# Experts: the activation issued behind the down projection's weights, and its 1 + tanh added on ScalarE

## The chip, the cores and the metric

The kernel runs on one core of a Trainium2 chip. The metric is the device time of one execution in microseconds (us). Five engines work side by side, each through its own row of instructions: TensorE (PE, matmuls; PEld are its weight loads), VectorE (DVE), ScalarE (ACT), GpSimd (POOL) and SyncE (SP, whose queue issues most transfers). An instruction waits by semaphores for what it needs, and whatever stands behind it on its engine waits with it.

## What is computed

The reference is two transformer blocks on 512 tokens of width 1024. The first has a layer of 32 experts, of which each token goes to 4; the change lies there. Cut to that:

```python
def expert_block(args):
    xblk, e = args
    gu = xblk @ w_gate_up[e] + b_gate_up[e]                 # [slots, 2048]
    gate = jnp.minimum(gu[:, :D_FF], SWIGLU_LIMIT)          # limit 7
    up = jnp.clip(gu[:, D_FF:], -SWIGLU_LIMIT, SWIGLU_LIMIT)
    act = (up + 1.0) * (gate * jax.nn.sigmoid(SWIGLU_ALPHA * gate))   # alpha 1.702
    return act @ w_down[e] + b_down[e]
...
out = jnp.zeros((t, d)).at[tbuf].add(ybuf * wbuf[:, None])
```

All of it is in float32, D_FF is 1024.

## The kernel before

**Products.** A float32 product is made of three matmuls (`mm3`, L82 to L84): both factors are split into a high and a low part, and high times low, low times high and high times high are summed in one bank of PSUM. A split is two instructions (`split`, L49 and L50): ScalarE copies the source to the high part (`whi`, `exh`), VectorE subtracts it from the source (`wlo`, `exl`). `ath` and `atl` are the same for the activation (L52, L53). So each weight tile passes through ScalarE, then VectorE, then TensorE.

**An expert.** Up to 96 token slots. Its weights are 12 tiles of 128x2048 (1 MB each), fetched by the SP queue into 8 raw buffers (L106), split into 4 buffers for high and 4 for low parts; each tile is 12 matmuls of 512 columns. An expert goes in two halves of the hidden width. A half has four tiles for its gate and up banks, here called a and b (the gate bank) and c and d (the up bank), each bank begun with a bias matmul (`add_bias`, L856), and then two tiles of a down product: in the first half of expert e that of the second half of expert e - 1 (called Yp0 and Yp1 here), in the second half that of its own first half (Yq0, Yq1). The loop over e in `moe` gives this order.

**The activation**, per half, at the end of `gate_up` (`g` is the gate bank): ScalarE makes `sg` = Relu(7 - g) (L889) and the Tanh of it (L890); VectorE clamps `up` (L893) and `gm` = min(g, 7) (L894), makes (sg + 1) * gm (L895) and (up + 1) * that (L896). sigmoid is had from the Tanh, and the factor 0.5 comes in at `ath`. Four transposes (`T<-ident,up`, L899) turn the result for the down product.

**Tokens.** `place` makes a one-hot matrix for an expert (`poh`, L772), four small matmuls give its token numbers (`T<-V`, L784, `gi` L785), four give its gates (`T<-VG`, L789; L791 copies two columns, L792 adds them). GpSimd gathers the tokens (`gather`, L796), `prep` transposes and splits them (L872, L49, L50). After an expert's last down tile ScalarE scales its two banks by the gates (`y`, L918) and GpSimd adds them to the output (`X`, L1009).

**What sets the order.** The engines take their instructions in a fixed order, found when the kernel is built: a scheduler with a modelled timeline takes what is ready by then, and what was written earlier in the text has precedence. So the order of the built program may differ from that of the text.

Of the kernel before, what the change touches and what calls it, by code (L numbers as in the profile page):

```python
# [9 lines left out]
F32 = mybir.dt.float32  # L10
# [4 lines left out]
AF = mybir.ActivationFunctionType  # L15
ALU = mybir.AluOpType
AX = mybir.AxisListType
# [12 lines left out]
NS = 96  # L30
# [4 lines left out]
def f(t):  # L35
    return t.bitcast(F32)


class Kern:
# [736 lines left out]
    def slots(self, bank, oh, V, vg, gi, gate):  # L776

        nc = self.nc
        n = oh.shape[-1]
        p = bank[:n, :4]  # L780

        def find():
            for i in range(NT):
                nc.tensor.matmul(p[:, :2], lhsT=oh[:, i], rhs=V[:, i], start=i == 0, stop=i == NT - 1)  # L784
            return nc.vector.tensor_scalar(gi[:n], p[:, 0:1], BASE, self.spare[:n], op0=ALU.add, op1=ALU.min).ins  # L785

        def gates():
            for i in range(NT):
                nc.tensor.matmul(p[:, 2:], lhsT=oh[:, i], rhs=vg[:, i], start=i == 0, stop=i == NT - 1)  # L789
            g = self.small.tile([128, 2], F32, name="g2")  # L790
            nc.vector.tensor_copy(g[:n], p[:, 2:])  # L791
            nc.vector.tensor_add(gate[:n], g[:n, 0:1], g[:n, 1:2])  # L792
        return find, gates

    def gather(self, e):
        self.nc.gpsimd.indirect_dma_start(out=self.xg[e % 2], out_offset=None, in_=self.XN[:, :],  # L796
                                          in_offset=bass.IndirectOffsetOnAxis(ap=self.gi[:NS, e:e + 1], axis=0),
                                          bounds_check=S - 1, oob_is_err=False)

    def moe_setup(self):  # L800

        nc, tc, a = self.nc, self.tc, self.a
        FF = 1024
        T = dict(reuse_waits="tile")
        self.ms = ExitStack()
        mc = self.mc = self.ms.enter_context(tc.tile_pool(name="mc", bufs=1, **T))
        xg = self.xg = [mc.tile([NS, D], F32, name=f"xg{n}") for n in range(2)]
        for t in xg:
            nc.gpsimd.memset(t, 0.0)
        self.mraw = self.ms.enter_context(tc.tile_pool(name="mraw", bufs=NE, **T))  # L810

        bias = self.bias = mc.tile([128, FF], F32R, name="bias")
        bt = self.mraw.tile([128, 2048], F32, name="bt", tag="raw")[:, :FF]
        for r in (0, 32):
            nc.sync.dma_start(bt[r:r + 32], a["b_gate_up"][:, :FF])
            nc.sync.dma_start(bt[64 + r:96 + r], a["b_gate_up"][:, FF:])
        nc.scalar.activation(bias, bt, AF.Copy)
        for r in (32, 96):  # L820
            nc.vector.tensor_sub(bias[r:r + 32], bt[r:r + 32], f(bias)[r:r + 32])

        esel = self.esel = mc.tile([128, 2, 32], F32R, name="esel")
        nc.gpsimd.memset(f(esel), 0.0)
        for r in range(0, 128, 32):
            nc.vector.tensor_copy(esel[r:r + 32, r // 64], self.ident[r:r + 32, r:r + 32])
        c7 = self.c7 = mc.tile([128, 2], F32, name="c7")
        nc.vector.memset(c7[:, 0:1], 7.0)
        nc.vector.memset(c7[:, 1:2], 0.851 * 7.0)
        self.gi = mc.tile([128, 32], I32, name="gi")  # L830
        self.gate = mc.tile([128, 32], F32, name="gate")

# [7 lines left out]
    def moe(self, ctx):  # L840


        nc, tc, a, mc = self.nc, self.tc, self.a, self.mc
        esel, bias, c7, xg = self.esel, self.bias, self.c7, self.xg
        E = 32
# [3 lines left out]
        mp = P("mp", 2, **T)  # L849
        self.wp, self.wk = (self.mraw, P("mhi", 4, **T), P("mlo", 4, **T)), 4  # L850
        psG, psY, psT = P("psG", 4, space=PSUM, **T), P("psY", 2, space=PSUM, **T), P("psTm", 2, space=PSUM, **T)
        gi, gate, gather = self.gi, self.gate, self.gather
        wgu, wdn = a["w_gate_up"], a["w_down"]

        def add_bias(ps, e, c):
            nc.tensor.matmul(ps, lhsT=esel[:, c // 2, e:e + 1].to_broadcast([128, NS]),  # L856
                             rhs=bias[:, c % 2 * 512:c % 2 * 512 + 512], start=True, stop=False)

        def place(e):

            for g in self.slots(psT.tile([128, 512], F32, name="T", tag="T"), self.onehot(mp, e), self.V,
                                self.VG[:, :, e], gi[:, e:e + 1], gate[:, e:e + 1]):
                g()

        def prep(e):
            xh = mp.tile([128, KT, NS], F32R, name="exh")
            xl = mp.tile([128, KT, NS], F32R, name="exl")
            for b in range(2):
                p = psT.tile([128, 512], F32, name="T", tag="T")[:, :4 * NS].rearrange("p (k s) -> p k s", k=4)
                for k in range(4):  # L870
                    c = (4 * b + k) * 128
                    nc.tensor.transpose(p[:, k], xg[e % 2][:, c:c + 128], self.ident[:NS, :NS])  # L872
                sl = slice(4 * b, 4 * b + 4)
                self.split(xh[:, sl], xl[:, sl], p)
            self.prep_dve = self.last_dve.ins
            return xh, xl

        def gate_up(e, h, x):
            xh, xl = x
            ps = []  # L880
            for c in (h, 2 + h):
                W = self.weight(wgu[e, :, c * 512:c * 512 + 512], KT, 512)
                p = psG.tile([128, 512], F32, name="G")[:NS]
                add_bias(p, e, c)
                self.mm3(p, [((xh[:, k], xl[:, k]), W[k]) for k in range(KT)], start=False)
                ps.append(p)
            s = mp.tile([NS, 512], F32, name="sg", bufs=3)

            nc.scalar.activation(s, ps[0], AF.Relu, scale=-1.0, bias=c7[:NS, 0:1])  # L889
            nc.scalar.activation(s, s, AF.Tanh, scale=-0.851, bias=c7[:NS, 1:2])  # L890
            u = mp.tile([NS, 512], F32, name="up", bufs=3)
            g = mp.tile([NS, 512], F32, name="gm", bufs=2)
            nc.vector.tensor_scalar(u, ps[1], 7.0, -7.0, op0=ALU.min, op1=ALU.max)  # L893
            nc.vector.tensor_scalar(g, ps[0], 7.0, None, op0=ALU.min)  # L894
            nc.vector.scalar_tensor_tensor(s, s, 1.0, g, op0=ALU.add, op1=ALU.mult)  # L895
            self.act_dve = nc.vector.scalar_tensor_tensor(u, u, 1.0, s, op0=ALU.add, op1=ALU.mult).ins  # L896
            p = psT.tile([128, 512], F32, name="T", tag="T")[:, :4 * NS].rearrange("p (k s) -> p k s", k=4)
            for k in range(4):
                nc.tensor.transpose(p[:, k], u[:, k * 128:(k + 1) * 128], self.ident[:NS, :NS])  # L899
            th = mp.tile([128, 4, NS], F32R, name="ath", bufs=3)  # L900
            tl = mp.tile([128, 4, NS], F32R, name="atl", bufs=3)
            self.split(th, tl, p, 0.5)
            return th, tl
# [3 lines left out]
        def down(e, h, t):  # L907
            th, tl = t
            if h == 0:
                yp[e] = [psY.tile([128, 512], F32, name="Y")[:NS] for c in range(2)]  # L910
            for c in range(2):
                W = self.weight(wdn[e, h * 512:h * 512 + 512, c * 512:c * 512 + 512], 4, 512,
                                parts=2 if e == E - 1 else 1)
                self.mm3(yp[e][c], [((th[:, k], tl[:, k]), W[k]) for k in range(4)], start=h == 0, stop=h == 1)
            if h == 1 and e < E - 1:
                y = mp.tile([NS, D], F32, name="y", bufs=1)
                for c in range(2):
                    nc.scalar.activation(y[:, c * 512:c * 512 + 512], yp[e][c], AF.Copy, scale=gate[:NS, e:e + 1])  # L918
                self.scatter(y, gi[:NS, e:e + 1])
# [31 lines left out]
        x = {0: prep(0)}  # L951
        acts = {}
# [2 lines left out]
        gather(1)  # L955
        place(2)
        for e in range(E):
            acts[e, 0] = gate_up(e, 0, x[e])
            if e + 1 < E:
                x[e + 1] = prep(e + 1)  # L960
                if e + 2 < E:
                    gather(e + 2)
                if e + 3 < E:
                    place(e + 3)
            if e == E - 4:
                gates_T()
            if e == E - 2:
                one_hot()
            if e:
                down(e - 1, 1, acts[e - 1, 1])  # L970
            acts[e, 1] = gate_up(e, 1, x[e])
            if e < E - 1:
                down(e, 0, acts[e, 0])

        with tc.issue_after(self.act_dve):
            down(E - 1, 0, acts[E - 1, 0])
# [4 lines left out]
        g = gate[:NS, E - 1:E]  # L981
# [561 lines left out]
```

## Time and profile before

| | us |
|---|---|
| median of 3 runs | 3069.35 |
| lowest, highest | 3063.36, 3070.2 |
| the profiled execution | 3069.6 |
| its span in the trace | 3067.8 |

Busy shares of the span: TensorE 95%, VectorE 73%, ScalarE 56%, GpSimd 9%. The experts take the stretch from about 730 to 1840 us. In the rows below a start is in us from the span's start, followed by the duration; a bracket holds the engine's idle time ahead of the instruction and what ended it. Matmuls overlap: what one costs is the distance from its start to the next start, not its duration. The same holds in a small way for ScalarE and VectorE, where an instruction can start a little before the one ahead ends.

### The profile page before, as it was taken

To read this page: it belongs to the slowest core of one execution; us is meant where nothing else is said; L and a number is where in the kernel's file an instruction comes from. 1 tells how busy PE (TensorE), PEld (TensorE's weight loads), DVE (VectorE), ACT (ScalarE), POOL (GpSimd) and SP (SyncE) were. 2 spreads that over 40 slices of the span, in tenths; PEclk is the share of its full clock that TensorE was granted. 3 is DMA by queue.
4 is the path that set the end of the run, shared out by engine and by line. 5 is a ranking of instruction groups with operands and counts; after the bars stand their busy time and mean duration, and the time that the engine had idled before them with its cause. 6 is when DMAs were issued, how large, how long until landed. Compare 5 with 4: busy or idle time off the path is not lost. (4 is left out here: it accounts for less than half of the span.)

```text
span 3067.8 us, 39458 instructions
## 1 busy us (share of the span) xinstructions
PE 2920.2 (95%) x14226; PEld 2296.0 (75%) x14226; DVE 2245.2 (73%) x3799; ACT 1732.8 (56%) x2569; POOL 290.5 (9%) x302
## 2 busy tenths in 40 slices
PE   8999999979999999999999998999999989999998
PEld 6898878766776666666666666778787868888877
DVE  7765677669999999999999997654456675445664
ACT  5545545337777777777777774444454234444632
POOL 0000001000112111111111100011001000110100
PEclk9999999989999999999999999999999999999999
DMA  4222233469999999999999994433536533345363
GB/s 158 63 63 67 82 105 101 140 252 335 368 364 340 357 354 356 359 358 360 356 358 359 348 371 139 127 98 112 122 92 209 165 93 116 112 115 114 92 228 99
DMA packets 406409, 644.93 MB, mean 210 GB/s; under 512 B 23088, under 2 KB 150592, under 8 KB 406208
## 3 DMA queue, kind: packets, MB, share of 16 engines
q1 hardware_dynamic: 386384, 581.67, 56.8%
q0 software_dynamic: 19248, 58.58, 6.5%
q8 instruction: 114, 1.87, 0.3%
q10 hardware_dynamic: 576, 2.10, 0.2%
q14 instruction: 87, 0.71, 0.1%
HBM read 592.10 MB, written 54.36 MB: 211 GB/s over the span
## 5 line engine op out<-in xcount | busy, mean ns | idle before, releaser
L50 DVE TENSOR_TENSOR wlo<-raw,whi 128x2048 fp32r<-128x2048 f32 (+3 forms) x646 | 1166.9, 1818 | 242.0 <-ACT whi L49 236.9
L49 ACT ACTIVATE whi<-raw 128x2048 fp32r<-128x2048 f32 (+3 forms) x646 | 972.5, 1532 | 233.0 <-PE M L84 110.0
L82 PE MATMUL G<-wlo,exh 128*96 128x512 f32 x1024 | 410.1, 400 | 4.8 <-ACT exh L49 2.8
L83 PE MATMUL G<-whi,exl 128*96 128x512 f32 x1024 | 403.9, 395 | 1.9 <-DVE exl L50 1.9
L84 PE MATMUL G<-whi,exh 128*96 128x512 f32 x1024 | 403.8, 395 | 0.0
L82 PE MATMUL F<-xl,whi 128*128 128x512 f32 x768 | 312.8, 407 | 17.4 <-DVE fl L1233 11.7
L83 PE MATMUL F<-xh,wlo 128*128 128x512 f32 x768 | 307.1, 400 | 1.5 <-DVE la L94 1.0
L84 PE MATMUL F<-xh,whi 128*128 128x512 f32 x768 | 307.4, 400 | 0.0
L82 PE MATMUL M<-wlo,xh 128*128 128x512 f32 (+2 forms) x736 | 279.0, 381 | 11.1 <-ACT xh L49 3.0
L83 PE MATMUL M<-whi,xl 128*128 128x512 f32 (+2 forms) x736 | 277.1, 377 | 3.7 <-DVE xl L50 3.1
L84 PE MATMUL M<-whi,xh 128*128 128x512 f32 (+2 forms) x736 | 275.3, 375 | 0.0
L84 PEld LDWEIGHTS G<-whi,exh 128*96 128x96 f32 x1024 | 165.6, 162 | 71.5
L82 PEld LDWEIGHTS G<-wlo,exh 128*96 128x96 f32 x1024 | 165.8, 162 | 70.6 <-ACT exh L49 3.0
L82 PE MATMUL Y<-wlo,ath 128*96 128x512 f32 x512 | 207.3, 405 | 10.7 <-DVE wlo L50 10.1
L83 PEld LDWEIGHTS G<-whi,exl 128*96 128x96 f32 x1024 | 165.7, 162 | 67.3 <-DVE exl L50 2.4
L83 PE MATMUL Y<-whi,atl 128*96 128x512 f32 x512 | 202.4, 395 | 0.1
L84 PE MATMUL Y<-whi,ath 128*96 128x512 f32 x512 | 201.8, 394 | 0.0
L82 PEld LDWEIGHTS M<-wlo,xh 128*128 128x128 f32 x736 | 165.1, 224 | 32.6 <-ACT xh L49 4.9
L82 PEld LDWEIGHTS F<-xl,whi 128*128 128x128 f32 x768 | 146.8, 191 | 54.0 <-DVE fl L1233 14.9
L83 PEld LDWEIGHTS M<-whi,xl 128*128 128x128 f32 x736 | 165.9, 225 | 18.9 <-DVE xl L50 4.0
L84 PEld LDWEIGHTS M<-whi,xh 128*128 128x128 f32 x736 | 165.4, 225 | 13.7
L84 PEld LDWEIGHTS F<-xh,whi 128*128 128x128 f32 x768 | 147.0, 191 | 32.1
(474 smaller groups left out, 5047.8 us busy)
## 6 DMA issues: line engine op xcount, KB each, us to landing
raw<-in_w_gate_up SPq DMA_DIRECT2D x256, 1024.0 KB, 7.1
raw<-in_w_down SPq DMA_DIRECT2D x124, 1024.0 KB, 8.1
raw<-in_w_in SPq DMA_DIRECT2D x154, 512.0 KB, 3.9
GZ<-fl POOLq DMA_DIRECT2D x80, 256.0 KB, 2.3
raw<-in_w_out SPq DMA_DIRECT2D x24, 512.0 KB, 3.8
raw<-in_w_branch SPq DMA_DIRECT2D x24, 512.0 KB, 4.0
gt<-GZ SPq DMA_DIRECT2D x48, 256.0 KB, 3.3
raw<-in_w_in SPq DMA_DIRECT2D x32, 256.0 KB, 3.0
```

What stands on the lines that cost most here:

```text
L49: self.last_act = nc.scalar.activation(hi, src, AF.Copy)
L50: self.last_dve = (eng or nc.vector).tensor_sub(lo, src, f(hi))
L82: nc.tensor.matmul(out, lhsT=ah, rhs=bl, start=start and i == 0, stop=False)
L83: nc.tensor.matmul(out, lhsT=al, rhs=bh, start=False, stop=False)
L84: self.last_mm = nc.tensor.matmul(out, lhsT=ah, rhs=bh, start=False, stop=stop and i == n - 1)
```

## The change

`gate_up` returns its two banks; a new function `act` makes the activation of them. It is called after the `down` that follows, in both halves, and `place(e + 3)` after the first of these calls. In `act`, ScalarE adds 1 to the Tanh by an Identity with a bias (a third column of the constants `c7`); VectorE then has min(g, 7) * sg as one instruction, the clamp of `up`, and (up + 1) * sg. In `slots`, one sum over two columns takes the place of a copy and an addition.

```diff
-            g = self.small.tile([128, 2], F32, name="g2")
-            nc.vector.tensor_copy(g[:n], p[:, 2:])
-            nc.vector.tensor_add(gate[:n], g[:n, 0:1], g[:n, 1:2])
+            nc.vector.reduce_sum(gate[:n], p[:, 2:], axis=AX.X)
...
+        c7 = self.c7 = mc.tile([128, 3], F32, name="c7")
...
+        nc.vector.memset(c7[:, 2:3], 1.0)
...
+            return ps
+
+        def act(ps):
             s = mp.tile([NS, 512], F32, name="sg", bufs=3)
 
             nc.scalar.activation(s, ps[0], AF.Relu, scale=-1.0, bias=c7[:NS, 0:1])
             nc.scalar.activation(s, s, AF.Tanh, scale=-0.851, bias=c7[:NS, 1:2])
+            nc.scalar.activation(s, s, AF.Identity, bias=c7[:NS, 2:3])
             u = mp.tile([NS, 512], F32, name="up", bufs=3)
-            g = mp.tile([NS, 512], F32, name="gm", bufs=2)
+            nc.vector.scalar_tensor_tensor(s, ps[0], 7.0, s, op0=ALU.min, op1=ALU.mult)
             nc.vector.tensor_scalar(u, ps[1], 7.0, -7.0, op0=ALU.min, op1=ALU.max)
-            nc.vector.tensor_scalar(g, ps[0], 7.0, None, op0=ALU.min)
-            nc.vector.scalar_tensor_tensor(s, s, 1.0, g, op0=ALU.add, op1=ALU.mult)
             self.act_dve = nc.vector.scalar_tensor_tensor(u, u, 1.0, s, op0=ALU.add, op1=ALU.mult).ins
...
         for e in range(E):
-            acts[e, 0] = gate_up(e, 0, x[e])
+
+            ps = gate_up(e, 0, x[e])
             if e + 1 < E:
                 x[e + 1] = prep(e + 1)
                 if e + 2 < E:
                     gather(e + 2)
-                if e + 3 < E:
-                    place(e + 3)
+            if e:
+                down(e - 1, 1, acts[e - 1, 1])
+            acts[e, 0] = act(ps)
+            if e + 3 < E:
+                place(e + 3)
...
-            if e:
-                down(e - 1, 1, acts[e - 1, 1])
-            acts[e, 1] = gate_up(e, 1, x[e])
+            ps = gate_up(e, 1, x[e])
             if e < E - 1:
                 down(e, 0, acts[e, 0])
+            acts[e, 1] = act(ps)
```

What the built order makes of it is seen at two places. The names in it are those of the code, with a number for each buffer; L891, L892 and L893 are Relu, Tanh and Identity after the change, L895 to L897 its three instructions on VectorE, L855 its bias matmul.

ScalarE, expert 20, first half, before: the copies of tiles a, b, c and d (the rows with `whi`, with `ath` between c and d), Relu, Tanh, and the copies of Yp0 and Yp1.

```order
L49 ACTIVATE whi_13022<-raw_13020 128x2048
L49 ACTIVATE whi_13028<-raw_13026 128x2048
L49 ACTIVATE whi_13060<-raw_13058 128x2048
L52 ACTIVATE ath_12978<-T_12973 128x384
L49 ACTIVATE whi_13066<-raw_13064 128x2048
L889 ACTIVATE sg_13096<-G_13032,c7_6252 96x512
L890 ACTIVATE sg_13096<-sg_13096,c7_6252 96x512
L49 ACTIVATE whi_13150<-raw_13148 128x2048
L49 ACTIVATE whi_13168<-raw_13166 128x2048
```

The same place after: a, b, two small copies, c, Relu, d, and so on to Yp1.

```order
L49 ACTIVATE whi_12937<-raw_12935 128x2048
L49 ACTIVATE whi_12943<-raw_12941 128x2048
L52 ACTIVATE ath_12931<-T_12926 128x384
L49 ACTIVATE exh_13011<-T_13013 128x384
L49 ACTIVATE whi_12975<-raw_12973 128x2048
L891 ACTIVATE sg_13072<-G_12947,c7_6252 96x512
L49 ACTIVATE whi_12981<-raw_12979 128x2048
L49 ACTIVATE exh_13011<-T_13020 128x384
L892 ACTIVATE sg_13072<-sg_13072,c7_6252 96x512
L49 ACTIVATE whi_13032<-raw_13030 128x2048
L893 ACTIVATE sg_13072<-sg_13072,c7_6252 96x512
L49 ACTIVATE whi_13050<-raw_13048 128x2048
```

Relu, which needs the finished gate bank, moved from behind the copy of d to ahead of it; Tanh stayed ahead of the first down tile, and Identity stands between the two down tiles.

TensorE, expert 19, second half, from the last matmuls of the up bank to the first down product, before:

```order
L82 MATMUL G_12938<-wlo_12935,exh_12510 96x512
L83 MATMUL G_12938<-whi_12934,exl_12511 96x512
L84 MATMUL G_12938<-whi_12934,exh_12510 96x512
L856 MATMUL G_13202<-bias_6237,esel_6246 96x512
L82 MATMUL Y_12982<-wlo_12987,ath_12808 96x512
```

And after, with the end of the first down tile and the start of the second below the dots:

```order
L82 MATMUL G_12854<-wlo_12851,exh_12415 96x512
L83 MATMUL G_12854<-whi_12850,exl_12416 96x512
L84 MATMUL G_12854<-whi_12850,exh_12415 96x512
L82 MATMUL Y_12880<-wlo_12885,ath_12787 96x512
...
L84 MATMUL Y_12880<-whi_12884,ath_12787 96x512
L855 MATMUL G_13114<-bias_6237,esel_6246 96x512
L855 MATMUL G_13152<-bias_6237,esel_6246 96x512
L82 MATMUL Y_12881<-wlo_12903,ath_12787 96x512
```

The bias matmul of a coming bank moved from ahead of the first down tile to behind it.

## Rows read from the trace of the kernel before

**Rows 1.** The page: busy time and share of the span, by engine.

```profile
PE 2920.2 (95%) x14226; PEld 2296.0 (75%) x14226; DVE 2245.2 (73%) x3799; ACT 1732.8 (56%) x2569; POOL 290.5 (9%) x302
```

**Rows 2.** Windows: length, each engine's busy time, granted clock, DMA share, GB/s.

```profile
804.52:877.06 72.54, 72.54 (x345) 51.62 (x344) 68.37 (x57) 56.01 (x45) 10.02 (x4) 1.00 1.04 367
1395.63:1469.97 74.34, 73.49 (x345) 51.23 (x344) 68.80 (x57) 55.19 (x44) 10.21 (x4) 1.00 1.03 358
711.20:714.20 3.00, 3.00 (x8) 1.93 (x7) 3.00 (x4) 0.00 (x0) 0.00 (x0) 0.50 1.05 374
```

**Rows 3.** Timeline, ScalarE: first copy of the results of experts 5 and 28.

```profile
913.35 0.69 ACT L918 ACTIVATE y<-Y,gate 96x512 f32<-96x512 f32 x1 [0.86 <-PE Y L84]
...
1768.18 0.69 ACT L918 ACTIVATE y<-Y,gate 96x512 f32<-96x512 f32 x1 [1.82 <-PE Y L84]
```

**Rows 4.** Waits from 1400 to 1550, SP's queue last: total, times, longest.

```profile
POOL X L1009 <- ACT y L918: 149.6, 5, 30.6
ACT sg L889 <- PE G L84: 13.4, 8, 3.3
...
SPq L106 <- DVE wlo L50: 121.0, 47, 4.4
```

**Rows 5.** Timeline, TensorE, both halves around expert 20's start.

```profile
1404.70 0.50 PE L872 MATMUL T<-ident,xg 96*128 96x96 f32 x4
1404.98 0.48 PE L784 MATMUL T<-V,poh 128*96 128x2 f32 x4
...
1412.37 0.47 PE L82 MATMUL Y<-wlo,ath 128*96 128x512 f32 x1 [0.71 <-DVE wlo L50]
1412.68 0.39 PE L83 MATMUL Y<-whi,atl 128*96 128x512 f32 x1
...
1424.10 0.40 PE L82 MATMUL G<-wlo,exh 128*96 128x512 f32 x1
...
1429.67 0.40 PE L856 MATMUL G<-bias,esel 128*96 128x512 f32 x1
1429.94 0.47 PE L82 MATMUL Y<-wlo,ath 128*96 128x512 f32 x1
```

**Rows 6.** Timeline, ScalarE, the same stretch.

```profile
1404.90 0.68 ACT L889 ACTIVATE sg<-G,c 96x512 f32<-96x512 f32 x1 [1.20 <-PE G L84]
1405.49 0.48 ACT L49 ACTIVATE exh<-T 128x384 fp32r<-128x384 f32 x1
1405.86 0.72 ACT L890 ACTIVATE sg<-sg,c 96x512 f32<-96x512 f32 x1
...
1424.30 0.69 ACT L889 ACTIVATE sg<-G,c 96x512 f32<-96x512 f32 x1 [3.25 <-PE G L84]
1425.02 0.73 ACT L890 ACTIVATE sg<-sg,c 96x512 f32<-96x512 f32 x1
1425.66 5.52 ACT L49 ACTIVATE whi<-raw 128x2048 fp32r<-128x2048 f32 x3
```

**Rows 7.** Timeline, VectorE, the same stretch.

```profile
1407.83 0.68 DVE L894 TENSOR_SCALAR gm<-G 96x512 f32<-96x512 f32 x1
1408.43 0.54 DVE L50 TENSOR_TENSOR exl<-T,exh 128x384 fp32r<-128x384 f32 x1
1408.90 0.15 DVE L791 COPY g<-T 96x2 f32<-96x2 f32 x1
...
1410.03 2.28 DVE L50 TENSOR_TENSOR wlo<-raw,whi 128x2048 fp32r<-128x2048 f32 x1
...
1427.59 2.29 DVE L50 TENSOR_TENSOR wlo<-raw,whi 128x2048 fp32r<-128x2048 f32 x1 [1.09 <-ACT whi L49]
```

**Rows 8.** Timeline, TensorE, outside the experts: matmuls after two longer waits.

```profile
709.48 0.45 PE L82 MATMUL G<-wlo,exh 128*96 128x512 f32 x1 [1.82 <-DVE wlo L50]
...
2047.22 0.50 PE L82 MATMUL F<-xl,whi 128*128 128x512 f32 x1 [2.39 <-DVE fl L1233]
2047.56 0.39 PE L83 MATMUL F<-xh,wlo 128*128 128x512 f32 x1
```

More of the change, by code (lines that the diff above doesn't have):

```diff
@@ L826, in moe_setup @@
             nc.vector.tensor_copy(esel[r:r + 32, r // 64], self.ident[r:r + 32, r:r + 32])
-        c7 = self.c7 = mc.tile([128, 2], F32, name="c7")
+        c7 = self.c7 = mc.tile([128, 3], F32, name="c7")
         nc.vector.memset(c7[:, 0:1], 7.0)
         nc.vector.memset(c7[:, 1:2], 0.851 * 7.0)
+        nc.vector.memset(c7[:, 2:3], 1.0)
         self.gi = mc.tile([128, 32], I32, name="gi")
```

## The prediction

> **What bounds the kernel now.** I read first the busy shares over the span, then the same shares in windows of the expert stage, since the span mixes stages with different limits. Over the span TensorE is busy 95%, VectorE 73%, ScalarE 56% [rows 1]. In the experts it is tighter: in two experts TensorE is busy 72.54 of 72.54 us early on and 73.49 of 74.34 us later, while VectorE is at 68.37 and 68.80 us and ScalarE at 56.01 and 55.19 us (the first two rows of [rows 2]). So TensorE sets the pace, VectorE has 2 to 3 us of slack per expert, ScalarE 8 to 10. The granted clock is 1.00 in both windows, that is 2.4 GHz. The DMA engines are full too, but no engine waits for them: the queue that fetches weights waits 121.0 us of 150 for VectorE to hand a raw buffer back [rows 4], so the fetches run ahead.
>
> What can be won in the experts is therefore TensorE's waits alone. TensorE's own work is 36.27 us per expert (72.54 for two, with no idle time [rows 2]). The first copy of an expert's result, on ScalarE, marks each expert: 913.35 us for expert 5, 1768.18 for expert 28 [rows 3]. That is 854.83 us for 23 experts; at 36.27 they would take 834.21. **20.6 us** of waits are there, and this is all that the change can remove.
>
> Where is it lost? At the first down tile of a half. At 1412.37 TensorE has waited 0.71 us for the low half of the down weights, and the matmul after the wait comes 0.31 later instead of the usual 0.23 [rows 5]; VectorE had made that half from 1410.03 for 2.28 us [rows 7]. One half later the same place is just met: VectorE itself waited 1.09 us for ScalarE's copy, and finished 0.04 us late. This second case shows the chain from the finished gate bank to the down product. Gate bank done at 1424.10 [rows 5]; Relu 0.20 later (1424.30), Tanh 0.72 after Relu (1425.02), the copy of the down weights 0.64 after that (1425.66) [rows 6], their low half 1.93 after the copy's start (1427.59) and 2.29 long [rows 7], the down product 0.06 later, at 1429.94: 5.84 us. Against it TensorE has the up bank's 24 matmuls and a bias, 5.57 and 0.23 (1424.10, 1429.67) [rows 5]. ScalarE spent 3.25 us before that Relu in waiting for the gate bank [rows 6]: it was not late, it stood in its place in the row.
>
> **The change, part by part.** (1) *The add of 1 on ScalarE.* Per half VectorE loses one of four instructions of 0.68 us, which in a row take 0.60 (1407.83 to 1408.43 [rows 7]). 64 halves make 38 us of VectorE's time, but VectorE is not what runs out; a half's saving counts only where it stands ahead of the low half of a down tile. ScalarE gains one of about 0.69. None of the rows shows an Identity; Relu, a plain pass with a bias, is the nearest, 0.68 and 0.69, and Tanh, at 0.72 and 0.73, is the other bound [rows 6]. Relu, Tanh and the copies already follow each other there without a pause that a change of function would need, so I take 0.69.
>
> (2) *The sum of two gate columns as one instruction.* It replaces two of 0.15 us, the first at 1408.90 [rows 7], on an engine with 2 us of slack; the bounds are 0.15 either way, 0 on the path.
>
> (3) *The new order.* In the text the activation now stands behind the down tiles, so one expects Relu and Tanh behind their weight copies. The order of the built kernel has that in experts 1 to 5 (and nearly in 6) only, where TensorE doesn't wait now either: worth 0. From 7 on it is different, and here the sum is made. I write times from the end of the gate bank; Relu starts at 0.20, and what follows it without needing it 0.59 later (1404.90, 1405.49 [rows 6]).
>
> *Eleven first halves* (experts 8, 10, ... 28) have Relu **ahead of the copy of d**, the last tile of the up bank. Before, d was copied long ahead: ScalarE then idled 3.25 us. Now d cannot start before 0.20 + 0.59 = 0.79; its low half starts 1.93 later and takes 2.29 (5.01), and the product starts 0.06 after it, at 5.07. TensorE is at d after four transposes (0.28: 1404.70 to 1404.98 [rows 5]) and c (12 matmuls, half of 5.57, so 2.79), plus an estimated 0.06 for the restart after transposes: 3.13. It waits 1.94, and the next matmul is 0.08 slower, as after 1412.37: **2.0 us, 22.0 in all**. The cover that d had, ScalarE's lead, is cut off by an instruction that waits in order; queued behind it are d, the second copy of the next tokens, Tanh and the down weights.
>
> *Five first halves* (11, 13, 19, 21, 27) have Relu, a copy of 0.37, Tanh, Identity and then the first down tile: 0.20 + 0.59 + 0.37 + 0.72 + 0.64 = 2.52; + 1.93 + 2.29 + 0.06 = 6.80, against 0.28 + 0.06 + 5.57 + 0.23 = 6.14: 0.66, **0.7 with the slower restart, 3.5 in all**. The 0.37 is what the small copy adds in a row (1405.49 to the next start at 1405.86).
>
> *Six first halves* (7, 9, 15, 17, 23, 25) meet the first down tile. The second is late. VectorE is through with the first one's low half at 0.20 + 0.72 + 0.64 + 1.93 + 2.29 = 5.78, and its next instruction starts 0.08 before that end (as 1408.43 stands to 1407.83), at 5.70. Ahead of the second low half now stand two instructions of the activation (0.60 each) and the small low half of the tokens (0.47: 1408.43 to 1408.90 [rows 7]): 5.70 + 1.20 + 0.47 + 2.29 + 0.06 = 9.72, against transposes, up bank, first tile and two biases, 0.34 + 5.57 + 2.79 + 0.46 = 9.16: **0.6, 3.6 in all**.
>
> *Thirteen second halves* (7, 9, ... 27, 29, 30) have Relu and Tanh ahead of the first down tile as before, so 5.84, but the bias matmul that filled 0.23 now stands behind that tile: 5.84 against 5.57, 0.27 and 0.08 more, and about 0.1 at the second down tile (two VectorE instructions ahead, 5.70 + 1.20 + 2.29 + 0.06 = 9.25, against 5.92 + 2.79 + 0.46 = 9.17): **0.45, 5.9 in all**. Other second halves have the copy of the down weights ahead of Tanh or of Relu: 0.
>
> *Rest:* 0.35 in the first halves of 29 and 30 (0.7), and 0.2 at the second down tile in six of the eleven, where again two VectorE instructions stand ahead (1.2). Sum of new waits: 22.0 + 3.5 + 3.6 + 5.9 + 0.7 + 1.2 = **36.9 us**. The old waits of 20.6 go, since no half keeps its old order. Net +16.3.
>
> (4) *The placing of tokens, moved behind the activation.* Its gather, scatter and small VectorE instructions come later on their queues: GpSimd now issues gathers in pairs. The scatter's queue has up to 30.6 us of waiting between its work [rows 4], and an expert's tokens are gathered two experts ahead; 0. If that cover went, one late gather would cost the few us of its landing, once.
>
> **The rivals.** *Faster:* VectorE is so full in the experts (93 to 94%) that the 0.6 us taken off per half ends the waits, and ScalarE is never at Relu before the bank is done. Then all 20.6 us go: 3069.6 - 20.6 = 3049.0. For it: TensorE's waits of today name VectorE. Against: the 3.25 us of idle ScalarE ahead of Relu, and 13.4 us in eight such waits [rows 4]; it decides if these are gone after the change. The Trainium skill, page "Perfetto Trace Analysis", section "Optimizing Scalar/DVE Operations", speaks for this rival: if VectorE is saturated, giving work to ScalarE may make sense. The windows show VectorE at 93 to 94% and not at its end, so the trace bears it out in part only.
>
> *Same:* only the eleven big waits come, the small ones (14.9) are absorbed by leads that I count too low: 22.0 - 20.6 = +1.4, 3071.0.
>
> *Slower still:* TensorE's granted clock falls after each of the eleven waits. After 1.82 us idle ahead of 709.48 [rows 8], from 711.20 on, eight matmuls took 3.00 us at a granted clock of 0.50, that is 1.2 GHz [rows 2]. At 0.2325 each they would have taken 1.86, so 1.14 were lost, and with the slower ones at its edges about 1.6; 11 x 1.6 = 17.6 on top, 3103. Against: after 2.39 us idle ahead of 2047.22 the matmul at 2047.56 takes 0.39 [rows 8].
>
> *The change doesn't do what it says:* that the activation still stands ahead of the down weights from expert 7 on is read from the built order and is part of the forecast, not a rival with a time of its own.
>
> **How the numbers follow.** The profiled execution took 3069.6 us around its span of 3067.8, 0.25 above the median of the runs (3069.35). 3069.6 + 16.3 = 3085.9, less 0.25: **3085.7**. Chances: this forecast 0.63, slower still 0.17, same 0.12, faster 0.08. The range goes from the same case's 3071.0, less 2 us since runs of the kernel before lie 7 us apart, to slower still: 3069 to 3104; it leaves out the faster case and a little at each end. A measurement tells about 0.2% (6 us) from no change. Faster by more 0.08, within 0.12, slower 0.80.
>
> **What would show it.** In the profile after: in the experts from 8 on, a wait of about 2 us of TensorE for VectorE's low half inside the up bank, every second expert, right behind a gate bank's end; ScalarE's idle time before Relu still there, 3 us; d's weight copy starting 0.6 us after Relu. Two experts take about 76 us instead of 74.3, experts 2 to 5 still 36.27 each. It is wrong if the waits inside the up bank are absent (then the order on the chip or ScalarE's lead isn't what I read), if they are 0.5 us or less, or if a stage outside the experts moves by more than 3 us.

## The result: 1.0% slower

The changed kernel takes 3099.55 us (median of 4 runs, 3096.08 to 3101.08), the kernel before 3069.77 (4 runs): ratio 1.0104, 95% interval 1.0091 to 1.0116. The direction and the main place are as forecast; the size, +29.8 us, is not: 16.3 were forecast.

The page of the changed kernel:

```profile
span 3097.9 us, 39364 instructions
...
PE 2937.5 (95%) x14226; PEld 2302.9 (74%) x14226; DVE 2200.6 (71%) x3704; ACT 1769.6 (57%) x2633; POOL 346.0 (11%) x302
```

Against [rows 1], VectorE did 44.6 us less work and ScalarE 36.8 more, which is what the edit says, and the span grew by 30.1. The busy shares tell nothing of why. The windows of the changed kernel do (columns as in [rows 2]: length, TensorE, weight loads, VectorE, ScalarE, GpSimd, clock, DMA share, GB/s):

```profile
882.71:955.44 72.73, 72.73 (x345) 51.66 (x344) 63.83 (x50) 56.74 (x48) 9.75 (x4) 1.00 1.02 354
1410.91:1486.88 75.97, 73.56 (x345) 51.10 (x344) 66.17 (x51) 57.36 (x48) 10.83 (x4) 1.00 1.02 349
1519.60:1522.60 3.00, 3.00 (x8) 1.95 (x9) 2.97 (x3) 3.00 (x4) 0.00 (x0) 0.53 0.60 170
```

Two early experts are free of idle time as before (72.73 us, before 72.54); two later ones take 75.97 us in place of 74.34, with 2.41 us of idle TensorE in place of 0.85, although VectorE has 2.6 us less to do in them. The third row is a stretch at half clock, to which I come below. The first copies of the results of experts 5, 28 and 30:

```profile
919.08 0.69 ACT L919 ACTIVATE y<-Y,gate 96x512 f32<-96x512 f32 x1 [0.26 <-PE Y L84]
...
1794.16 0.69 ACT L919 ACTIVATE y<-Y,gate 96x512 f32<-96x512 f32 x1 [1.22 <-PE Y L84]
...
1866.47 0.68 ACT L919 ACTIVATE y<-Y,gate 96x512 f32<-96x512 f32 x1 [1.19 <-PE Y L84]
```

And that of expert 30 in the kernel before, beside [rows 3]:

```profile
1839.73 0.69 ACT L918 ACTIVATE y<-Y,gate 96x512 f32<-96x512 f32 x1 [1.83 <-PE Y L84]
```

These rows cut the 30.1 us into four parts: expert 5 comes 5.7 later, the stretch from 5 to 28 takes 875.08 us in place of 854.83 (+20.3), that from 28 to 30 takes 0.8 more, and what lies behind 30 takes 1231.4 in place of 1228.1 (+3.4).

**The wait in the experts.** TensorE in the first half of expert 20, at the last product of tile c and the first of d:

```profile
1441.47 0.39 PE L84 MATMUL G<-whi,exh 128*96 128x512 f32 x1
1443.64 0.47 PE L82 MATMUL G<-wlo,exh 128*96 128x512 f32 x1 [1.79 <-DVE wlo L50]
1443.95 0.39 PE L83 MATMUL G<-whi,exl 128*96 128x512 f32 x1
```

The next start is 2.17 us away instead of 0.23: 1.94 lost, and 0.08 with the slower matmul behind the wait. The engine named is VectorE. Its row shows that it was not the cause, for it waited itself, and ScalarE's rows, under it, show what for:

```profile
1441.30 2.29 DVE L50 TENSOR_TENSOR wlo<-raw,whi 128x2048 fp32r<-128x2048 f32 x1 [3.40 <-ACT whi L49]
```

```profile
1433.64 1.92 ACT L49 ACTIVATE whi<-raw 128x2048 fp32r<-128x2048 f32 x1
1438.77 0.69 ACT L891 ACTIVATE sg<-G,c 96x512 f32<-96x512 f32 x1 [3.20 <-PE G L84]
1439.36 1.91 ACT L49 ACTIVATE whi<-raw 128x2048 fp32r<-128x2048 f32 x1
...
1443.95 0.72 ACT L893 ACTIVATE sg<-sg,c 96x512 f32<-96x512 f32 x1
```

ScalarE copies c, then stands 3.20 us with Relu at the head of its row until TensorE ends the gate bank, and only then copies d, whose raw weights it could have read all the while (e1 below copies c and d in one go). So TensorE waits for VectorE, VectorE for ScalarE, and ScalarE for TensorE. The last row is the Identity: 0.72 us, nearer to Tanh than to the 0.69 that I took. Eleven such waits, 1.94 to 1.97 us each, stand in the experts from 8 on. In the sums of waits from 1400 to 1550, ScalarE's wait for the gate bank did not shrink (13.4 us before [rows 4]), VectorE's for ScalarE's copies was 5.1 us before, and the last two rows are new:

```profile
ACT sg L891 <- PE G L84: 15.3, 8, 3.2
DVE wlo L50 <- ACT whi L49: 13.3, 12, 3.4
...
PEld G L82 <- DVE wlo L50: 4.5, 2, 2.2
PE G L82 <- DVE wlo L50: 3.6, 2, 1.8
```

**The clock.** Behind two of the eleven waits TensorE goes on at half clock. At the next one of them:

```profile
1517.43 0.39 PE L84 MATMUL G<-whi,exh 128*96 128x512 f32 x1
1519.60 0.63 PE L82 MATMUL G<-wlo,exh 128*96 128x512 f32 x1 [1.79 <-DVE wlo L50]
1520.03 0.63 PE L83 MATMUL G<-whi,exl 128*96 128x512 f32 x1
```

The wait has the same length as that of 1443.64, but matmuls are 0.43 apart instead of 0.23 until 1523, with the granted clock at 0.53 (the third window above), that is mostly at 1.2 GHz. By the starts, such a stretch costs 1.2 to 1.5 us, the two together 2.7, without the 0.08 that follows each wait.

### The profile page after: what moved, and what is told of

Same layout as the page of the kernel before. It is cut to its first block, busy times and chain, and to the rows that moved or that the text cites. A ratio compares the mean times of both kernels' runs of the same rounds, so it can differ in the third digit from the quotient of the medians.

```text
span 3097.9 us, 39364 instructions
## 1 busy us (share of the span) xinstructions
PE 2937.5 (95%) x14226; PEld 2302.9 (74%) x14226; DVE 2200.6 (71%) x3704; ACT 1769.6 (57%) x2633; POOL 346.0 (11%) x302
## 4 chain that ended last, share of the span: by engine, by line
PE 75%; DVE 9%; issue 7%; ACT 6%; DMA 3%; SPq 0%; POOL 0%; DVEq 0%; ACTq 0%; POOLq 0%
PE M L82 7%; PE M L83 6%; PE M L84 6%; PE G L82 6%; PE G L84 6%; PE G L83 6%; PE F L82 6%; PE F L83 5%; PE F L84 5%; DVE wlo L50 4%; PE Y L82 4%; PE Y L83 4%; PE Y L84 4%; ACT whi L49 3%; DMA raw<-in_w_in 1%
## 5 line engine op out<-in xcount | busy, mean ns | idle before, releaser
L82 PE MATMUL G<-wlo,exh 128*96 128x512 f32 x1024 | 412.9, 403 | 23.3 <-DVE wlo L50 20.6
L84 PEld LDWEIGHTS G<-whi,exh 128*96 128x96 f32 x1024 | 166.7, 163 | 71.4
L1013 POOL DMA_INDIRECT X<-y,gi x31 | 121.6, 3921 | 592.6 <-ACT y L919 589.0
L82 PEld LDWEIGHTS F<-xl,whi 128*128 128x128 f32 x768 | 146.9, 191 | 54.2 <-DVE fl L1237 13.4
```

What stands on the lines that cost most here:

```text
L82: nc.tensor.matmul(out, lhsT=ah, rhs=bl, start=start and i == 0, stop=False)
L84: self.last_mm = nc.tensor.matmul(out, lhsT=ah, rhs=bh, start=False, stop=stop and i == n - 1)
L1013: self.nc.gpsimd.indirect_dma_start(out=self.X1[:, :], out_offset=bass.IndirectOffsetOnAxis(ap=rows, axis=0), in_=y, in_offset=None, bound ...
```

## Experiments

The theory to test (theory 1): the place of Relu and its fellows in ScalarE's row sets the time in the experts. Rivals: the added load on ScalarE (theory 2), and VectorE's load. Besides, 9 us lie outside the experts. Each run's span, cut at the first copies of the results of experts 5, 28 and 30 as above (us):

| run | until expert 5 | 5 to 28 | 28 to 30 | behind 30 | span | median of runs |
|---|---|---|---|---|---|---|
| before | 913.4 | 854.8 | 71.6 | 1228.1 | 3067.8 | 3069.8 |
| changed | 919.1 | 875.1 | 72.3 | 1231.4 | 3097.9 | 3099.6 |
| e1 Relu behind d | 915.9 | 853.0 | 72.4 | 1228.8 | 3070.1 | 3071.8 |
| e2 all behind the down tiles | 919.6 | 838.3 | 70.9 | 1230.1 | 3058.9 | 3060.3 |
| e3 move only | 913.7 | 866.5 | 70.8 | 1229.2 | 3080.2 | 3081.9 |
| e4 arithmetic only | 922.4 | 858.3 | 72.5 | 1229.2 | 3082.5 | 3084.2 |
| e5 as e2, old arithmetic | 919.2 | 854.2 | 72.5 | 1229.0 | 3074.8 | 3073.8 |
| e6 as e2, expert 28 mended | 920.3 | 835.0 | 70.3 | 1228.5 | 3054.0 | 3055.0 |
| f1 changed, 64 bytes on | 913.1 | 878.1 | 72.4 | 1230.0 | 3093.5 | 3094.1 |
| f2 as e6, 64 bytes on | 914.9 | 835.6 | 70.3 | 1227.0 | 3047.7 | 3049.0 |
| f3 gate sum only | 918.9 | 853.4 | 71.4 | 1227.0 | 3070.7 | 3070.3 |

**e1: Relu behind the copy of d.** One instruction is queued behind another; no arithmetic changes.

```diff
-            return ps
+            return ps, self.last_act.ins
 
         def act(ps):
+            ps, d = ps
...
-            nc.scalar.activation(s, ps[0], AF.Relu, scale=-1.0, bias=c7[:NS, 0:1])
+            with tc.issue_after(d):
+                nc.scalar.activation(s, ps[0], AF.Relu, scale=-1.0, bias=c7[:NS, 0:1])
```

> The changed kernel, with Relu queued behind the copy of d, the up bank's last weight tile, on ScalarE. Theory 1 (the place of Relu in ScalarE's row): the eleven waits of 1.95 us inside the up bank and the clock halvings behind two of them (2.9 us) go; these eleven halves then get the 0.3 to 0.7 us wait at the first down tile that their neighbours have, so about 24.4 - 5 = 19 us less than the changed kernel: 3080 us. Theory 2 (ScalarE carries one instruction more per half, and that load is what costs): the order of one instruction makes little difference, 3095 to 3100 us.

3071.81 us, ratio to before 1.0008 (0.9999 to 1.0018). ScalarE's rows in a first half show c and d copied in one go ahead of Relu, and the idle time there fallen to 1.39 us:

```profile
1382.93 3.73 ACT L49 ACTIVATE whi<-raw 128x2048 fp32r<-128x2048 f32 x2
1388.05 0.69 ACT L893 ACTIVATE sg<-G,c 96x512 f32<-96x512 f32 x1 [1.39 <-PE G L84]
1388.63 0.48 ACT L49 ACTIVATE exh<-T 128x384 fp32r<-128x384 f32 x1
```

The waits inside the up bank are gone, no stretch in the experts is at half clock, and the experts from 5 to 28 take 22.1 us less than in the changed kernel. With Identity still there, theory 2 is out as the cause of the large loss. The total fell by 27.7 where I expected 19: 5.8 of it stand outside the experts (below).

**e3: the move alone**, with Relu ahead of d in the same eleven halves, and **e4: the arithmetic alone**. In e3 the lines of Identity and of the new VectorE product go back to the four old instructions, and the gates to copy and addition; in e4 those lines and the sum are put into the kernel before.

> Only the move: the activation written behind the down projection, and the placing behind it, with the arithmetic of before (no Identity, four instructions on VectorE, copy and addition for the gates). Its row on ScalarE has Relu ahead of the copy of d in eleven first halves too. Theory 1: nearly the whole loss is here, 3088 to 3100 us, with a wait of about 1.95 us in these eleven halves. Theory 2: about the kernel before, 3066 to 3075 us.

> Only the arithmetic: Identity on ScalarE, three instructions on VectorE and one sum for the gates, with the activation where it was before in the text. On ScalarE Relu stays behind d, Tanh ahead of the first down tile, Identity between the two down tiles. Theory 1: 0.3 us at each first down tile and 0.1 at each second, about 0.8 us per expert against 0.9 in the kernel before: 3064 to 3072 us. Theory 2 (the added instruction on ScalarE costs): 0.7 us more per half, 3085 to 3105 us.

e3: 3081.93 us (ratio 1.0036, 1.0022 to 1.0051). The waits are there, in the window from 1400 to 1550, somewhat shorter (1.74 us by the starts) as a bias matmul lies between c and d:

```profile
PEld G L82 <- DVE wlo L50: 4.1, 2, 2.0
...
PE G L82 <- DVE wlo L50: 3.1, 2, 1.6
```

It is less than I expected: experts 5 to 28 lose 11.7 us to before, not 20. Of the 8.6 by which the changed kernel is worse, 2.7 are the half clock, which follows none of the eleven waits here, and 2.4 the shorter waits; the other 3.5 were not followed one by one. e4: 3084.24 us (1.0054, 1.0036 to 1.0071), far over my 3064 to 3072. But its loss is not where theory 2 puts it: experts 5 to 28 take 3.5 us more than before, and 9.0 of its 14.7 us stand ahead of the copy for expert 5, most of it ahead of the experts, in code that is the same; why so much is lost there stays open. In the experts from 5 to 28, then, the move alone costs 11.7 us, the arithmetic alone 3.5, and 5.1 of the 20.3 come only with both together.

**e2: the activation where the change's text has it**, behind the copy of the second down tile in ScalarE's row, in every half.

```diff
-            nc.scalar.activation(s, ps[0], AF.Relu, scale=-1.0, bias=c7[:NS, 0:1])
+            with tc.issue_after(self.last_act.ins):
+                nc.scalar.activation(s, ps[0], AF.Relu, scale=-1.0, bias=c7[:NS, 0:1])
```

> The changed kernel, with Relu, Tanh and Identity queued on ScalarE behind the copy of the second down tile in every half, as the text of the change reads. Theory 1: no wait of TensorE for weights is left in experts 2 to 30, 36.3 us each as experts 2 to 5 have now; 31 us of waits and 2.9 us of slow clock go, 3062 to 3068 us, so below the kernel before if the 9 us that the changed kernel lost outside the experts come back, and about equal to it if not. Theory 2 (load on ScalarE): waits stay, over 3085 us. A third (VectorE, with its three instructions and the token work, is the bound when ScalarE is not): 36.9 to 37.2 us per expert, 3075 to 3085 us.

3060.32 us, ratio 0.9970 (0.9960 to 0.9980): faster than both kernels, and a little below the 3062 to 3068 that I expected. Two experts take 72.51 us, with no idle time of TensorE:

```profile
1391.30:1463.81 72.51, 72.51 (x346) 51.60 (x345) 65.83 (x51) 57.26 (x50) 15.10 (x4) 1.00 1.05 366
```

One wait is left in the experts from 5 to 28, in expert 28: TensorE, and ScalarE's row around it:

```profile
1720.08 0.39 PE L84 MATMUL Y<-whi,ath 128*96 128x512 f32 x1
1722.39 0.51 PE L82 MATMUL G<-wlo,exh 128*96 128x512 f32 x1 [1.93 <-DVE wlo L50]
```

```profile
1715.15 1.05 ACT L936 ACTIVATE bdn<-bt 96x1024 fp32r<-96x1024 f32 x1
1716.10 0.71 ACT L893 ACTIVATE sg<-sg,c 96x512 f32<-96x512 f32 x1
1717.52 0.68 ACT L920 ACTIVATE y<-Y,gate 96x512 f32<-96x512 f32 x1 [0.71 <-PE Y L84]
1718.11 1.91 ACT L49 ACTIVATE whi<-raw 128x2048 fp32r<-128x2048 f32 x1
```

A copy of the down projection's biases for the end of the experts (`bdn`, made in `gates_T()`) and the copy of a result, which waits, stand ahead of the next weight copy.

**e5: the same order with the old arithmetic** (e3 with the edit of e2) asks whether VectorE's relief is worth anything.

> Relu and Tanh queued behind the copy of the second down tile on ScalarE, as in the run before of that kind, but with the arithmetic of the kernel before: no Identity, four instructions on VectorE. Theory 1 (ScalarE's row alone): 36.25 us per expert as in that run, 3055 to 3064 us in all, and the lighter VectorE was worth nothing there. Rival (VectorE's relief is what makes that order hold): 36.5 to 37 us per expert, 3066 to 3080 us.

3073.80 us, ratio 1.0011 (1.0001 to 1.0022), and 37.02 us per expert: the rival holds. TensorE waits at the first gate tile of 22 of the 23 experts between these copies, and VectorE's row ahead of it is full:

```profile
1439.54 0.40 PE L857 MATMUL G<-bias,esel 128*96 128x512 f32 x1
1440.45 0.47 PE L82 MATMUL G<-wlo,exh 128*96 128x512 f32 x1 [0.51 <-DVE wlo L50]
```

```profile
1434.25 2.28 DVE L50 TENSOR_TENSOR wlo<-raw,whi 128x2048 fp32r<-128x2048 f32 x1
1436.45 0.68 DVE L899 TENSOR_SCALAR gm<-G 96x512 f32<-96x512 f32 x1
1437.05 0.54 DVE L50 TENSOR_TENSOR exl<-T,exh 128x384 fp32r<-128x384 f32 x1
1437.51 0.68 DVE L900 SCALAR_TENSOR_TENSOR sg<-sg,gm 96x512 f32<-96x512 f32 x1
1438.11 2.28 DVE L50 TENSOR_TENSOR wlo<-raw,whi 128x2048 fp32r<-128x2048 f32 x1
```

No bracket: VectorE waits for nobody here. Three instructions stand between two weight tiles, and the one that the change takes away (0.60 with the pause) is about the wait (0.65 to 0.69 by the starts, but for one of 2.0 in expert 28). In this order VectorE is the bound, and the lighter arithmetic is worth 37.02 - 36.25 = 0.77 us per expert; in the order that the changed kernel was built with it is worth nothing: there experts 5 to 28 take 875.1 us with it and 866.5 without (e3). The Trainium skill, page "Perfetto Trace Analysis", section "Optimizing Scalar/DVE Operations", says that work may be given to ScalarE if VectorE is saturated. The two runs agree with it, with one addition: VectorE's 92% over two experts (68.35 of 74.06 us in e5) was enough, once ScalarE's order no longer came first.

**e6: expert 28 mended.** As e2, but expert 0's first half is left free, and `gates_T()` is called one half later.

> The changed kernel with Relu, Tanh and Identity behind the second down tile, except in expert 0's first half, and with the preparation of the gates for the last expert moved one half later, so that its copy on ScalarE no longer stands ahead of a weight copy in expert 28. Expected: the wait of 2.08 us in expert 28 and the 1.56 us of slow clock behind it go, one or two us in experts 0 and 1: 3054 to 3060 us. If what is lost outside the experts belongs to each built program by chance, the time may be 3 to 6 us off either way.

3054.98 us, ratio 0.9956 (0.9939 to 0.9973). Experts 5 to 28 take 3.3 us less than in e2; ahead of expert 5 nothing was won. In 797 us of experts TensorE is never idle:

```profile
920.00:1717.00 797.00, 797.00 (x3783) 567.11 (x3782) 720.81 (x549) 626.65 (x527) 167.34 (x47) 1.00 1.04 364
```

**e7 to e12: both kernels again.** The stretches outside the experts hold instructions that the change does not touch; these executions ask if their times belong to the program.

> The changed kernel once more, for the stretch ahead of the experts. If the stretches at half clock belong to the program, the 4.5 us it was behind at 660 us come again, at the same places. If they fall by chance, they come elsewhere and the delay at 660 us lies anywhere from 0 to 6 us.

> The kernel before once more. If the stretches at half clock belong to the program, they come where they came (12.8, 429.7, 711.2 us) and the first result copy at 732 us. If by chance, elsewhere, and that copy comes up to 6 us later.

> The kernel before, a third look, for the stretches outside the experts: its first result copy of expert 5 stood at 913.4 and 914.4 us, its end 1228.1 and 1227.7 us behind that of expert 30. If the program sets these, 913 to 915 and 1227 to 1229 again; if chance does, values of the changed kernel (917 to 919, 1229 to 1231) may appear.

> The changed kernel, a third look: expert 5 at 919.1 and 917.1 us so far, end 1231.4 and 1228.6 us behind expert 30, experts 5 to 28 in 875.1 and 874.9 us. If the program sets it, 917 to 919 again; if chance does, 913 to 919. The experts are to take 875 us again, with half clock behind the same two waits.

> The kernel before, a fourth look, as the third: 913 to 915 us for expert 5 if the program sets it, up to 919 if chance does.

> The changed kernel, a fourth look, as the third: 917 to 919 us for expert 5 if the program sets it, 913 to 919 if chance does.

| us, four executions each | until expert 5 | 5 to 28 | 28 to 30 | behind 30 |
|---|---|---|---|---|
| before | 913.4, 914.4, 913.0, 913.3 | 854.8, 854.7, 854.7, 854.6 | 71.5 each | 1228.1, 1227.7, 1223.6, 1229.2 |
| changed | 919.1, 917.1, 917.6, 915.9 | 875.1, 874.9, 874.8, 878.1 | 72.3 to 72.4 | 1231.4, 1228.6, 1232.7, 1230.3 |
| difference of means | 3.9 | 21.0 | 0.85 | 3.6 |

The experts repeat within 0.3 us, but for the number of half-clock stretches in the changed kernel: 2, 2, 2 and 4, each behind one of the eleven long waits. Outside, executions of one kernel differ by 1 to 6 us. Ahead of expert 5 the two kernels still stand apart (at most 914.4 and at least 915.9 us): something there belongs to the program. Behind expert 30 they overlap (1229.2 and 1228.6), so these 3.6 us are not shown to.

**f1: the buffers moved by 64 bytes, and nothing else.** The old gates had a small buffer `g2`; without it the pool of small tiles is 64 bytes shorter, and all that is allocated behind it lies nearer to the start of the memory. f1 is the changed kernel with that buffer kept, unused; each engine has the same instructions in the same order.

```diff
+            self.small.tile([128, 2], F32, name="g2")
             nc.vector.reduce_sum(gate[:n], p[:, 2:], axis=AX.X)
```

> The changed kernel, instruction for instruction in the same order on every engine, with an unused buffer of the name g2 kept in the pool of small tiles, so that all that is allocated behind it lies 64 bytes further on, where it lay in the kernel before. If the place of the buffers sets the distance of matmuls outside the experts, that goes back from 230.7 to 227.5 ns (products into S, ahead of the experts) and from 232.5 to 231.4 ns (products into F, behind them), and expert 5 comes at 914 to 916 us in place of 917.4: 3 to 5 us less, about 3095 us. If not, 3099 us with the same distances as the changed kernel.

3094.10 us (3090.7 to 3096.0) against 3099.55. The first matmuls of a product ahead of the experts, in the summary of their lines (count; shortest, median and longest duration in ns; first and last start), in the kernel before:

```profile
L82 PE MATMUL S<-kzl,whi x24: 387/389/394, 557.4 to 596.2; 128*128 128x512 f32 x24
```

in the changed kernel:

```profile
L82 PE MATMUL S<-kzl,whi x24: 388/396/398, 559.9 to 599.8; 128*128 128x512 f32 x24
```

and in f1:

```profile
L82 PE MATMUL S<-kzl,whi x24: 387/389/394, 558.2 to 597.0; 128*128 128x512 f32 x24
```

The same stretch takes 38.8, 39.9 and 38.8 us, with no wait in it and the clock at full. The mean distance of starts of 512-column matmuls of one product without a wait (distances from 220 to 240 ns) is 227.6, 230.6 and 227.6 ns for products into S ahead of the experts, 231.3, 232.4 and 231.4 ns for those into F behind them. The other runs bear it out: that stretch takes 38.8 us in all eight executions of programs that keep `g2` (before, e3, e5, f1, f2) and 39.9 in all nine of those that dropped it (changed, e1, e2, e4, e6, f3). So the place of the buffers sets this distance, and 1.1 us of the 3.9 ahead of expert 5. Expert 5 comes at 913.1, as in the kernel before, but that is one execution, and what makes up the rest of the 3.9 was not followed: half clock comes and goes there, and e5, with `g2` kept, begins this stretch at 561.7 us, the kernel before at 557.4 to 558.8. Behind the experts the time fell by only 0.8 us from the changed kernel's mean; F is back at its distance there, while M (231.9 to 232.4 ns in the kernel before) and the half-clock stretches differ between executions of one kernel. That rest of about 3 us stays open.

**f2: e6 with the same 64 bytes.**

> The version with the activation behind the down projection's second tile, 3055 us, with the same 64 bytes kept. If the place of the buffers costs what it seems to: 3050 to 3052 us; if not, 3055 us.

3049.01 us, ratio 0.9933 (0.9913 to 0.9954): the fastest. Its runs (3047.8 to 3049.5) all lie below those of e6 (3052.3 to 3060.0), while the kernel before took 3069.3 and 3068.8 us beside them; so the 64 bytes are worth about 6 us here, and 5.5 in f1. The page and the window of the experts:

```profile
span 3047.7 us, 39363 instructions
```

```profile
915.00:1713.10 798.10, 798.10 (x3785) 567.72 (x3784) 721.39 (x549) 627.66 (x526) 165.08 (x47) 1.00 1.04 363
```

**f3: the gate sum alone, in the kernel before.**

> The kernel before with one sum in place of copy and addition for the gates, and nothing else; the buffers lie 64 bytes nearer, and the built order changes in places. If the place of the buffers costs 3 to 4 us outside the experts, 3070 to 3076 us; the instruction itself is worth nothing. If not, 3068 to 3071 us.

3070.26 us, ratio 1.0005 (0.9993 to 1.0017). Expert 5 is 5.5 us later and S stands at 230.8 ns, as the theory has it; but the experts take 1.4 us less, the part behind them is not longer, and the sum is within the measurement. On what the place of the buffers costs in all, this run doesn't decide.

## Where the prediction held, and where it was wrong

The bound, the order of the rows and the wait of 2.0 us held. The sum of 16.3 us failed in what it put at nothing: the stages outside the experts, which take 7.5 us more, and the clock, 3.4; small waits add 2.9. That 3099.55 lies in the range, and near the 3103 of "slower still", is luck: of the 17.6 us of that rival's mechanism 3.4 came.

*The bound, and what can be won* (right). TensorE's waits in the experts, 20.6 us, are what there is to win: e6 and f2 have none and take 36.25 to 36.3 us per expert. f2 gained about 20 in all, though not by the order that the change was built with.

*Relu ahead of d, 2.0 us eleven times* (right). Measured 1.94 to 1.97 and 0.08; e1 took them away.

*The smaller waits* (right in kind, a little short). Five first halves were to have 0.7 and have 0.67 to 0.71; five of six were to have 0.6 and have 0.53 to 0.56; second halves have 0.24 to 0.29 at the first down tile, as worked out. In the experts from 5 to 28 TensorE's time over 36.27 per expert is 875.08 - 834.21 = 40.9 us; less 2.7 for the clock, 38.2 against 35.3 forecast for this stretch (36.9 less 1.6 for experts 29 and 30). The 2.9 were not followed one by one; a wait of 0.6 at 1760.44 is among them, and experts without a wait take 36.37 us here (72.73 for two), not the 36.27 that were to stay.

*Identity at 0.69* (0.72) and *the gate sum at nothing* (0.154 us as one instruction): right as instructions. But the sum's edit did cost something, see below: it was priced as an instruction, not by the buffer that it drops.

*The clock* (the step that failed first). I had it fall after none of the waits, or, as a rival, after all eleven for 17.6 us. It fell after 2, 2, 2 and 4 of them in four executions, and after 4 in f1: 14 of 55, some 2.7 to 5.7 us in each. The rival's mechanism was real; as all or nothing it was the wrong form, and an expected share of it belonged into the sum.

*Outside the experts, nothing* (the step that failed most). I forecast no change there, and said that a move by more than 3 us would make the prediction wrong. By the means it is 3.9 ahead of expert 5 and 3.6 behind the experts, 7.5 of the missing 13 us. f1 and f2 showed one cause, in an edit that I had priced at nothing: dropping a buffer of a few bytes moved all that are allocated behind it, which is worth 5.5 and 6.0 us of the whole time. Followed to the matmuls are 1.1 us of it; how the rest divides over the stages stays open.

Put together from the means of the four executions: 16.3 forecast, + 2.9 small waits, + 3.4 clock, + 7.5 outside, - 0.7 in the last experts, is 29.4, the difference of the means.

*The rivals.* "Faster" was to be decided by ScalarE's idle time ahead of Relu: it stayed at 3.20 us, and the rival fell. Its premise was sound in another order, as e2 and e5 show. "The change doesn't do what it says" I took as part of the forecast, and that was the heart of it: from expert 7 on the built program has the activation, or part of it, ahead of the down tiles.

## To carry to other kernels

Where an instruction waits for the engine that sets the pace, look at what stands behind it in its own row: work that could have been done during the wait is lost time two engines further on. Moving lines in the text of a scheduled program is a wish; read the built order, and pin the one place that matters (e2's single line turned +1.0% into -0.3%). Before an edit is called free, ask what it does to the addresses of everything else, and compare stages that it doesn't touch.

## What the runs showed of the hardware

Matmuls of 512 columns at full clock, with no wait between, stand 226.7 or 233.3 ns apart (12 in 2.72 or 2.80 us) in the same code ahead of the experts, and the place of the buffers, moved by 64 bytes, decides which. Which operand's place it is was not tried. The first matmuls of two products that follow each other, 12 matmuls apart, in the kernel before and then in the changed one:

```profile
568.31 0.39 PE L82 MATMUL S<-kzl,whi 128*128 128x512 f32 x1
...
571.03 0.39 PE L82 MATMUL M<-kzl,whi 128*128 128x512 f32 x1
```

```profile
565.49 0.39 PE L82 MATMUL S<-kzl,whi 128*128 128x512 f32 x1
...
568.29 0.39 PE L82 MATMUL M<-kzl,whi 128*128 128x512 f32 x1
```

A wait of 1.77 to 1.82 us of TensorE was followed by half clock in 14 of 55 cases (five executions of two programs with the same instructions), and by full clock in the others. Which of the eleven it was changed from one execution to the next, so the program alone doesn't decide it. In the one execution of e3 none of eleven waits, 0.2 us shorter, was followed by it.
